# A two-layer transformer block on one core: six weight slots instead of four share the beginning with the first modulation

## The chip, the core and the metric

The kernel runs as one program on one core of a Trainium2 chip (trn2). The metric is the time of one execution in microseconds (us) of the device. The engines are TensorE (PE in the profile; its weight loads stand apart as PEld), VectorE (DVE), ScalarE (ACT), GpSimd (POOL) and SyncE (SP). Each engine takes its instructions in the order in which the program issued them; that order is written out by the kernel itself, since the code runs under a manual schedule. SP's queue issues nearly all transfers.

## What is computed

The reference is a transformer of two layers on 256 tokens of an image and 256 tokens of context, 1024 wide. Each layer has a half feed-forward step, an attention step and a second half feed-forward step. Nine vectors of modulation per layer come from a product of two conditioning vectors with `w_ada`. Cut to what the change touches:

```python
mod_x = (silu(c) @ w_ada[l] + b_ada[l]).reshape(bn, 1, N_MOD, d)
mod_c = (silu(c_ctx) @ w_ada[l] + b_ada[l]).reshape(1, 1, N_MOD, d)

def _half_ffn(h, g, shift, scale, gate, w_up, w_down):
    y = _rmsnorm(h, g) * (1 + scale) + shift
    a, b = split(y @ w_up, 2)            # w_up: 1024 x 5632
    return h + 0.5 * gate * ((silu(a) * b) @ w_down)

h_x = _half_ffn(h_x, norm_g[l, 0], mod_x[:, :, 0], mod_x[:, :, 1], mod_x[:, :, 2], ffn1_up[l], ffn1_down[l])
h_c = _half_ffn(h_c, norm_g[l, 0], mod_c[:, :, 0], mod_c[:, :, 1], mod_c[:, :, 2], ffn1_up[l], ffn1_down[l])
# then attention with mod 3, 4, 5 and the second half feed-forward with mod 6, 7, 8
```

All inputs are fp32, and the first up projection can't start before the shift and scale (modulation rows 0 and 1) of its first columns are known.

## The kernel before, in words

**Products.** Activations and weights are each kept as a high part (fp32r) and a low part, the remainder. A *unit product* is one TensorE instruction on a 128 x 128 weight tile and 512 tokens (256 in the parts that go by halves of the tokens). Three of them make one step of a projection's sum: high weight by high activation, high by low, low by high (`mm3`, L349 to L351). A projection of 1024 inputs has 8 such steps, so a column block of 128 outputs takes 24 unit products.

**Weight slots.** The weights come as a stream of loads of 1 MB (`raw`, three buffers, `RAW_BUFS`). One load makes two *slots* of 1024 columns: ScalarE casts the high part (L307), VectorE subtracts to get the low part (L310). Seven buffers hold slots (`W_BUFS`). `pump` casts ahead while fewer than six are out, `take` hands the next slot to a projection and casts it on the spot if it isn't there yet, `done` gives a slot back and pumps. What is cast ahead, and so where a cast stands on ScalarE and VectorE, is thus fixed when the program is built, by a count of slots that are out. For the first feed-forward, each load has 128 columns of both halves of `ffn1_up`, in rows of 512 bytes (`ffn_stream`).

**The planner's clock.** `tick` adds a planned duration to a clock of the program's own at every step of products, and runs what `later` has put off until then: the squares and sums for the norm of the next stage, pieces of modulation, refills. The place of such work in the engines' orders comes from this clock.

**The beginning.** Rows 0 and 1 of the modulation are computed in four *quarters* of 256 columns. A quarter has two loads of 1 MB (`quarter_load`, i = 0 and 1), two groups of four TensorE products (`quarter_ada`, L1306), a copy on ScalarE (L240), four transposes (`quarter_finish`, L1313), a reduction on VectorE (L1315) and then four modulations, for two chunks of 128 features and two sets of 256 tokens: VectorE makes the scaled value (L438), ScalarE the high part (L439), VectorE the low part (L433). A quarter so releases two of the eight steps of the up projection. `first` (L1356) handles the first four slots in this rhythm: the four PSUM banks of the `mm` pool hold one output block each, and quarters 1, 2 and 3 stand between the steps that are already released. The table `AT` says how many of the four blocks run ahead of a quarter's products and of its transposes. The four slots come out of the common stream (`take`): the transfers of the first two loads go to two pieces of the input buffer that are free by then (`extra`), and the two loads of quarter 0 stand ahead of both of them. `emit_split(lambda: quarter_finish(0, sb))` casts the first slot ahead of quarter 0's modulations.

**The other modulation rows.** Rows 2, 3, 4, 5 and 8 of layer 0 (`MODS[0]`) are accumulated during the first half feed-forward, one piece of 512 columns and 128 inputs at a time (`ada_one`: a load of 256 KB, and a multiply-add on VectorE, L222). `ada_step` is called after every up slot outside `first` and after every down slot: 40 times there (44 up slots without the first four) and 22 times in the down projections, 62 in all. Each call allows two pieces as long as the urgent row 2 is worked on, and 1.3 after that (`ADA_RATE`). When a row is complete, its sum across partitions, `ada_total` (L230), follows 22 us of the planner's clock later (`ADA_TOT`), 5 us for the urgent row. The accumulator lies in one of the seven slot buffers until that sum is made, so a fourth slot of what comes next can't be cast before it.

**The boundary to attention.** The last down chunks are followed by the squares (L375), the statistics (L411, L390 to L399) and the modulations of attention's operand, first for tokens 0 to 255, then for the rest. `attention` takes four slots at its start (L797).

```python
sl = [take() for _ in range(4)]     # L797, attention's first four slots
```

Of the kernel before, what the change touches and what calls it, by code (L numbers as in the profile page):

```python
# [32 lines left out]
AT = ((1, 2), (0, 1), (0, 1))  # L33
# [18 lines left out]
def dit_kernel(  # L52
# [515 lines left out]
    def ffn(a, gate, both, after, split_first, prep=None, mods=(), each=None):  # L568
# [4 lines left out]
        for pi, (f0, nf) in enumerate(FPARTS):  # L573
# [674 lines left out]
    ffn_stream(ffn1_up[0], ffn1_down[0])  # L1248
# [6 lines left out]
    with tc.manual_schedule():  # L1255
# [12 lines left out]
        extra += [xin[:, 4096:6144], xin[:, 6144:8192]]  # L1268

# [30 lines left out]
        def quarter_ada(h):  # L1300
# [3 lines left out]
            for i in range(2):  # L1304
                for j in range(4):
                    PE.matmul(out=ps[32 * j:32 * j + 32, :], lhsT=sc[:, 4 * i + j, :], rhs=raws[2 * h + i][:, j * 512:(j + 1) * 512],  # L1306
                              start=(i == 0), stop=(i == 1))
            return ada_rows(ps)

        def quarter_finish(h, sb):  # L1310
            tp = ps_ada.tile([128, 512], F32, tag="ada", name="ada")
            for q in range(4):
                PE.transpose(tp[:, q * 128:(q + 1) * 128], sb[:, q * 128:(q + 1) * 128], ident)  # L1313
            part = small.tile([128, 40], F32, tag="rs_t", name="part")[:, 0:8]
# [30 lines left out]
        sb = quarter_ada(0)  # L1345
# [3 lines left out]
        for v in range(2):  # L1349
            rstds[v] = r4[:, 2 * v:2 * v + 2]  # L1350
            ups.append(apply(v, 0, a["t"], None, spread(v, rb[:, v * TX:v * TX + TX])))
        raws += [quarter_load(1, 1, xv[:, 0:2].rearrange("p b d -> p (b d)")), quarter_load(2, 0, xv[:, 2:4].rearrange("p b d -> p (b d)"))]
        raws += [quarter_load(h, i, fresh()) for h, i in ((2, 1), (3, 0))]
        emit_split(lambda: quarter_finish(0, sb))

        def first():  # L1356

            ps = [mm_bank() for _ in range(4)]

            def dense(h, js):  # L1360
                for k in (2 * h, 2 * h + 1):
                    for j in js:
                        mm3(ps[j], [(wcol(sl[j], k, 0), acol(a["t"], k, 0, NT))], NT, k == 0, k == KD - 1)
            sl = [take() for _ in range(4)]
            for h in range(3):
                dense(h, range(0, AT[h][0]))
                sb = quarter_ada(h + 1)
                if h == 0:
                    raws.append(quarter_load(3, 1, fresh()))
                else:  # L1370
                    st["raws"] -= 1
                    loads()
                dense(h, range(AT[h][0], AT[h][1]))
                quarter_finish(h + 1, sb)
                dense(h, range(AT[h][1], 4))
            st["raws"] -= 1
            loads()
            for i in range(2):
                dense(3, (2 * i, 2 * i + 1))
                done(2)  # L1380
            return ps
# [117 lines left out]
```

## Time and profile before

| | |
|---|---|
| runs of the kernel before, us | 1706.02, 1703.14, 1705.49; median 1705.49 |
| the profiled execution, us | 1705.38 |
| its span in the trace, us | 1703.6 |
| mean granted clock of TensorE | 0.994 of full speed |
| TensorE busy | 1672.7 us, 98% |
| VectorE busy | 1037.6 us, 61% |
| ScalarE busy | 670.7 us, 39% |

The profiled execution's own time is 1.8 us longer than its span, which is what lies around the instructions. Busy times are sums over instructions; TensorE's matmuls overlap one another in the records, so a unit product shows about 0.36 us though one ends every 0.23. The 40 slices of the page show full busy shares nearly everywhere; the first slice is the one that stands out, with TensorE busy in six tenths of it, and the granted clock there in eight.

### The profile page before, as it was taken

How to read it: one execution, taken by the hardware profiler on the slowest of the kernel's cores; microseconds unless marked ns; L12 is line 12 of the kernel's file. 1: busy time of each engine (PE TensorE's matmuls, PEld its weight loads, DVE VectorE, ACT ScalarE, POOL GpSimd, SP SyncE). 2: the span in 40 equal slices, each digit the busy share in tenths (PEclk: the TensorE clock that was granted, in tenths of full speed). 3: DMA queues.
4: the chain of work that ended last, by engine and by line, in shares of the span. 5: the costliest groups of instructions: out<-in, count | busy, mean ns of one | idle time of the engine just before them, and what ended most of it. 6: DMA issues, size and time to landing. Idle time of an engine off the chain costs nothing.

```text
span 1703.6 us, 23729 instructions
## 1 busy us (share of the span) xinstructions
PE 1672.7 (98%) x9512; PEld 1417.9 (83%) x9512; DVE 1037.6 (61%) x1781; ACT 670.7 (39%) x1135; POOL 47.6 (3%) x67
## 2 busy tenths in 40 slices
PE   6999999999999999999999999999999999999998
PEld 4778888889886798888888898888888997799998
DVE  4666667567555676665764466545533657586674
ACT  4432222324556743323233243213222356674443
POOL 0000200000010000000000000020000000010000
PEclk8999999999999999999999999999999999999999
DMA  9745556432304325553653325565533224566561
GB/s 320 205 162 173 173 161 191 154 128 66 112 25 167 108 74 185 173 149 121 194 155 120 91 81 175 159 174 167 148 99 99 75 76 162 172 198 181 167 198 50
DMA packets 295335, 246.48 MB, mean 145 GB/s; under 512 B 9377, under 2 KB 262442, under 8 KB 293176
## 3 DMA queue, kind: packets, MB, share of 16 engines
q1 hardware_dynamic: 292680, 241.30, 45.8%
q0 software_dynamic: 1088, 2.15, 0.5%
q8 instruction: 75, 1.23, 0.3%
q10 hardware_dynamic: 1456, 1.52, 0.3%
q14 instruction: 36, 0.29, 0.1%
HBM read 243.88 MB, written 2.00 MB: 144 GB/s over the span
## 4 chain that ended last, share of the span: by engine, by line
PE 90%; DVE 4%; DMA 3%; ACT 2%; issue 1%; SPq 0%; DVEq 0%; ACTq 0%
PE mm L349 25%; PE mm L350 25%; PE mm L351 25%; PE mm L645 2%; PE mm L644 2%; PE mm L646 2%; PE mm L1010 1%; PE aux L976 1%; DMA ada_raw<-in_w_ada_dram 1%; DVE w L310 1%; PE ada L182 1%; PE mm L936 1%; DVE ada_acc L222 1%; PE mm L937 1%; PE ada L230 1%
## 5 line engine op out<-in xcount | busy, mean ns | idle before, releaser
L349 PE MATMUL mm<-act,w 128*128 128x512 f32 (+1 forms) x2240 | 809.8, 362 | 3.6 <-ACT act L439 2.1
L351 PE MATMUL mm<-act,w 128*128 128x512 f32 (+1 forms) x2240 | 802.7, 358 | 1.9 <-DVE w L310 1.9
L350 PE MATMUL mm<-act,w 128*128 128x512 f32 (+1 forms) x2240 | 802.9, 358 | 1.1 <-DVE act L433 0.9
L310 DVE TENSOR_TENSOR w<-raw,w 128x1024 fp32r<-128x1024 f32 (+1 forms) x311 | 369.9, 1198 | 219.4 <-ACT w L307 218.4
L349 PEld LDWEIGHTS mm<-act,w 128*128 128x128 f32 x2240 | 424.1, 189 | 84.8 <-issue 16.8
L351 PEld LDWEIGHTS mm<-act,w 128*128 128x128 f32 x2240 | 424.1, 189 | 64.2 <-DVE w L310 2.5
L350 PEld LDWEIGHTS mm<-act,w 128*128 128x128 f32 x2240 | 424.4, 189 | 62.8 <-DVE act L433 1.4
L307 ACT CAST w<-raw 128x1024 fp32r<-128x1024 f32 (+1 forms) x312 | 315.4, 1025 | 119.4 <-PE mm L351 96.9
L222 DVE SCALAR_TENSOR_TENSOR ada_acc<-ada_raw,sc,ada_acc 128x512 f32<-128x512 f32 x308 | 216.1, 746 | 50.3 <-DMA ada_raw<-in_w_ada_dram 26.2
L564 ACT CAST act<-gf 128x512 fp32r<-128x512 f32 x66 | 40.9, 620 | 275.5 <-DVE gf L561 275.5
L463 DVE SCALAR_TENSOR_TENSOR hT<-mm,hgt,hT 128x256 f32<-128x256 f32 x168 | 75.1, 480 | 95.9 <-PE mm L351 95.6
L558 ACT ACTIVATE sil<-mm 128x512 f32<-128x512 f32 x66 | 39.4, 597 | 185.5 <-PE mm L351 185.4
L645 PE MATMUL mm<-act,w 128*128 128x258 f32 x352 | 99.5, 283 | 0.3 <-DVE act L620 0.2
L644 PE MATMUL mm<-act,w 128*128 128x258 f32 x352 | 99.8, 284 | 0.0
L646 PE MATMUL mm<-act,w 128*128 128x258 f32 x352 | 99.3, 282 | 0.0
L561 DVE TENSOR_TENSOR gf<-sil,mm 128x512 f32<-128x512 f32 x66 | 45.2, 686 | 81.4 <-PE mm L351 70.8
L565 DVE TENSOR_TENSOR act<-gf,act 128x512 fp32r<-128x512 f32 x66 | 45.7, 693 | 45.3 <-ACT act L564 45.3
L645 PEld LDWEIGHTS mm<-act,w 128*128 128x128 f32 x352 | 66.8, 190 | 0.8 <-DVE act L620 0.8
L644 PEld LDWEIGHTS mm<-act,w 128*128 128x128 f32 x352 | 66.5, 189 | 0.0
L646 PEld LDWEIGHTS mm<-act,w 128*128 128x128 f32 x352 | 66.3, 188 | 0.0
L375 ACT ACTIVATE sq<-hT 128x256 f32<-128x256 f32 (+1 forms) x52 | 25.5, 490 | 102.5 <-DVE hT L463 102.2
L439 ACT ACTIVATE act<-nt,modT 128x256 fp32r<-128x256 f32 x80 | 39.5, 507 | 40.5 <-DVE nt L438 40.4
(171 smaller groups left out, 1163.4 us busy)
## 6 DMA issues: line engine op xcount, KB each, us to landing
raw<-in_ffn_up_dram SPq DMA_DIRECT2D x172, 512.0 KB
ada_raw<-in_w_ada_dram SPq DMA_DIRECT2D x192, 256.0 KB
raw<-in_ffn_down_dram SPq DMA_DIRECT2D x32, 1024.0 KB
raw<-in_w_ada_dram SPq DMA_DIRECT2D x16, 1024.0 KB
raw<-in_ffn_down_dram SPq DMA_DIRECT2D x16, 768.0 KB
raw<-in_w_in_dram SPq DMA_DIRECT2D x10, 1024.0 KB
raw<-in_w_out_dram SPq DMA_DIRECT2D x8, 1024.0 KB
raw<-in_w_ada_dram SPq DMA_DIRECT2D x12, 512.0 KB
```

What stands on the lines that cost most here:

```text
L222: DVE.scalar_tensor_tensor(out=o, in0=raw, scalar=col, in1=o, op0=ALU.mult, op1=ALU.add)
L307: ACT.copy(out=wh, in_=sl)
L310: eng.tensor_tensor(out=wl, in0=sl, in1=wh.bitcast(F32), op=ALU.subtract)
L349: PE.matmul(out=ps, lhsT=wh, rhs=ah, start=start and i == 0, stop=False)
L350: PE.matmul(out=ps, lhsT=wh, rhs=al, start=False, stop=False)
L351: PE.matmul(out=ps, lhsT=wl, rhs=ah, start=False, stop=stop and i == last)
L463: DVE.scalar_tensor_tensor(out=hT[:, k, cols], in0=ps, scalar=gate[:, k, v:v + 1], in1=hT[:, k, cols], op0=ALU.mult, op1=ALU.add)
L561: DVE.tensor_tensor(out=u[:, 0:n], in0=s[:, 0:n], in1=pb[:, 0:n], op=ALU.mult)
L565: DVE.tensor_tensor(out=gl, in0=uv, in1=gh.bitcast(F32), op=ALU.subtract)
L644: PE.matmul(out=ps[:, 0:NX], lhsT=wh, rhs=ah, start=k == 0, stop=False)
L645: PE.matmul(out=ps[:, 0:NX], lhsT=wh, rhs=al, start=False, stop=False)
L646: PE.matmul(out=ps[:, 0:NX], lhsT=wl, rhs=ah, start=False, stop=k == KD - 1)
```

## The change

`first` now handles six slots and not four: five banks of the `mm` pool and one of the `aux` pool hold the outputs (`ps6`), and the order of steps is written out by hand.

- **Loads.** The first two loads of the stream are 256 columns of each half of `ffn1_up`, in rows of 1 KB (`ffn_stream(..., wide=2)`); each makes two slots of one half. The loads of blocks and of quarters alternate: block 0 stands ahead of quarter 1, block 1 between the two loads of quarter 1 and quarter 2, block 2 (still 512-byte rows) ahead of quarter 3. `block(2)` reuses the buffer of block 0, so it waits for the casts of slots 0 and 1.
- **Casts.** `early_part` casts part of a slot: 256 columns (two of eight steps) and then 768 for slots 0 to 3, twice 512 for slots 4 and 5. The first slots' parts stand in front of quarter 0's modulations, not the whole first slot. Slots 2 and 3 are cast behind quarter 1's modulations, slots 4 and 5 behind quarter 2's.
- **TensorE's order.** The products of two blocks alternate (`dense`), and quarter 1 comes after 12 of them, as before after 12 of two blocks. `busy(n)` puts n small products of the identity with itself at five places of the beginning (4, 2, 8, 2 and 8 of them); their result is overwritten. The factors of the norm (`factors`, the transposes of the reciprocal roots) stand between the two halves of quarter 0.
- **The rest of the feed-forward.** `first` yields three pairs of banks; after each pair's evacuation `done(2)` gives two slots back. Two more slots pass without an `ada_step`, so 60 calls are left of 62.

```diff
-AT = ((1, 2), (0, 1), (0, 1))
...
             if "products" in a and pi == 0:
-                pss = a["products"]()
-                for i in range(2):
-                    up_evac(pss[2 * i], pss[2 * i + 1], g, i, 1, 0, n)()
-                m = 2
+                for pa, pb in a["products"]():
+                    up_evac(pa, pb, g, m, 1, 0, n)()
+                    done(2)
+                    m += 1
...
-    def ffn_stream(up, down):
+    def ffn_stream(up, down, wide=0):
...
+        for o in (0, DFF) if wide else ():
+            add_main(up[:, o:o + 256].rearrange("(k p) f -> p k f", p=128), (KD, 256), [c0, c1])
         for f0, nf in FPARTS:
-            for fj in range(f0 * 128, (f0 + nf) * 128, 128):
+            for fj in range((f0 or wide) * 128, (f0 + nf) * 128, 128):
...
-        raws = [quarter_load(0, i, fresh()) for i in range(2)]
-        loads()
-        raws.append(quarter_load(1, 0, fresh()))
+        def block(i):
+            extra.append(xin[:, 4096 + i % 2 * 2048:6144 + i % 2 * 2048])
+            emit_load()
+        raws = {(0, i): quarter_load(0, i, fresh()) for i in range(2)}
+        block(0)
+        raws[1, 0] = quarter_load(1, 0, fresh())
...
+        def busy(n):
+            for _ in range(n):
+                PE.matmul(out=ps6[-1][:, 0:128], lhsT=ident, rhs=ident, start=True, stop=True)
...
+        def early_part(j, k0, k1):
+            sl = slots[("raw", j // 2)][:, 0:2048].rearrange("p (k c) -> p k c", k=KD)[:, k0:k1, j % 2 * 128:(j % 2 + 1) * 128]
...
+            ACT.copy(out=wh, in_=sl)
+            return lambda: DVE.tensor_tensor(out=wl, in0=sl, in1=wh.bitcast(F32), op=ALU.subtract)
...
-        emit_split(lambda: quarter_finish(0, sb))
+        sb = quarter_ada(0, factors)
+        busy(2)
+        raws[1, 1] = quarter_load(1, 1, xv[:, 0:2].rearrange("p b d -> p (b d)"))
+        block(1)
+        raws[2, 0] = quarter_load(2, 0, xv[:, 2:4].rearrange("p b d -> p (b d)"))
+        raws[2, 1] = quarter_load(2, 1, fresh())
+        low0, low1 = early_part(0, 0, 2), early_part(1, 0, 2)
+        low0()
+        quarter_finish(0, sb, 8)
+        low1()
+        early_pair(0, 2, KD)
+        block(2)
+        raws[3, 0] = quarter_load(3, 0, fresh())
...
+            dense(0, 0, 1)
+            sb = quarter_ada(1)
+            raws[3, 1] = quarter_load(3, 1, fresh())
+            busy(2)
+            quarter_finish(1, sb, 8)
+            early_pair(2, 0, 2)
+            early_pair(2, 2, KD)
+            dense(1, 0, 1)
+            dense(0, 2, 3)
+            sb = quarter_ada(2)
...
+            dense(1, 2)
+            quarter_finish(2, sb)
+            early_pair(4, 0, 4)
+            early_pair(4, 4, KD)
+            dense(1, 3)
+            dense(0, 4, 5)
+            dense(2, 0, 1)
+            sb = quarter_ada(3)
...
+            dense(1, 4)
+            quarter_finish(3, sb)
+            dense(1, 5)
+            dense(2, 2, 3)
+            dense(2, 4, 5)
...
+            for pa, pb in ((0, 2), (1, 3), (4, 5)):
+                dense(3, pa, pb)
+                yield ps6[pa], ps6[pb]
```

**How the orders differ.** The first place is ScalarE's order from the casts behind quarter 0 to quarter 2's modulations, in the kernel before. The names `w_` are slots, `xin` and `raw` the buffers of the loads, `adasb` the copy of a quarter, `act` the first operand's high parts.

```order
L307 CAST w_265<-xin_103 128x1024
L307 CAST w_268<-xin_103 128x1024
L307 CAST w_271<-xin_103 128x1024
L240 COPY adasb_289<-ada_280 128x512
L439 ACTIVATE act_217<-nt_309,modT_94 128x256
L439 ACTIVATE act_217<-nt_312,modT_94 128x256
L439 ACTIVATE act_217<-nt_315,modT_94 128x256
L439 ACTIVATE act_217<-nt_319,modT_94 128x256
L240 COPY adasb_346<-ada_337 128x512
L439 ACTIVATE act_217<-nt_366,modT_94 128x256
```

In the kernel before, the casts of slots 1 to 3 stand ahead of quarter 1's copy, and no cast stands between the quarters. In the changed kernel the place from quarter 2's copy on reads:

```order
L239 COPY adasb_392<-ada_383 128x512
L438 ACTIVATE act_203<-nt_412,modT_94 128x256
L438 ACTIVATE act_203<-nt_415,modT_94 128x256
L438 ACTIVATE act_203<-nt_418,modT_94 128x256
L438 ACTIVATE act_203<-nt_422,modT_94 128x256
L1330 CAST w_428<-xin_103 128x512
L1330 CAST w_430<-xin_103 128x512
L1330 CAST w_428<-xin_103 128x512
L1330 CAST w_430<-xin_103 128x512
L239 COPY adasb_477<-ada_468 128x512
```

The four casts of slots 4 and 5 (`w_428`, `w_430`) stand behind all four modulations of quarter 2 and ahead of quarter 3's copy.

The second place is TensorE's order around quarter 2 in the changed kernel; `mm_206` and `mm_207` are the outputs of slots 2 and 3, `mm_208` and `aux_209` those of slots 4 and 5.

```order
L1404 MATMUL mm_207<-act_203,w_351 128x512
L1310 MATMUL ada_383<-xin_103,sc_93 32x512 x4
L1310 MATMUL ada_383<-raw_236,sc_93 32x512 x4
L1404 MATMUL mm_206<-act_203,w_349 128x512 x6
L1340 MATMUL ada_403<-ident_85,adasb_392 128x128 x4
L1404 MATMUL mm_207<-act_203,w_351 128x512 x6
L1404 MATMUL mm_208<-act_203,w_428 128x512
L1404 MATMUL aux_209<-act_203,w_430 128x512
```

Six products stand on either side of the transposes, and the products that come next are those of slots 4 and 5 with quarter 0's features. In the kernel before, the products behind quarter 2's transposes (L1313) were those of slots that had been cast before quarter 1.

The third place is ScalarE's order at the end of the first half feed-forward, in the kernel before. `sq` are the squares of the last down chunks, `w_2820`, `w_2853`, `w_2888` and `w_2915` attention's first four slots, `adasb_2913` is the copy of the fifth modulation row's sum.

```order
L307 CAST w_2820<-raw_2641 128x1024
L375 ACTIVATE sq_2851<-hT_84 128x512
L307 CAST w_2853<-raw_2641 128x1024
L375 ACTIVATE sq_2886<-hT_84 128x512
L307 CAST w_2888<-raw_2717 128x1024
L240 COPY adasb_2913<-ada_2907 128x512
L307 CAST w_2915<-raw_2717 128x1024
L375 ACTIVATE sq_2931<-hT_84 128x256
L375 ACTIVATE sq_2960<-hT_84 128x256
```

The same place in the changed kernel; attention's first four slots are `w_2851`, `w_2886`, `w_2921` and `w_3074`, the fifth is `w_3142`, and `adasb_3140` is the copy of the fifth row's sum.

```order
L374 ACTIVATE sq_2980<-hT_84 128x256
L374 ACTIVATE sq_3027<-hT_84 128x256
L438 ACTIVATE act_3039<-nt_3043,modT_94 128x256
L438 ACTIVATE act_3039<-nt_3055,modT_94 128x256
L438 ACTIVATE act_3039<-nt_3066,modT_94 128x256
L374 ACTIVATE sq_3071<-hT_84 128x256
L306 CAST w_3074<-raw_2738 128x1024
L438 ACTIVATE act_3039<-nt_3098,modT_94 128x256
L438 ACTIVATE act_3039<-nt_3132,modT_94 128x256
L438 ACTIVATE act_3039<-nt_3136,modT_94 128x256
L239 COPY adasb_3140<-ada_3108 128x512
L306 CAST w_3142<-raw_2817 128x1024
```

The fourth cast has moved behind the last square and into the modulations, and the fifth row's copy and a fifth cast have moved behind six modulations.

## Rows read from the trace of the kernel before

**Rows 1.** Part 1 of the page: busy time, share of the span, instructions.
```profile
PE 1672.7 (98%) x9512; PEld 1417.9 (83%) x9512; DVE 1037.6 (61%) x1781; ACT 670.7 (39%) x1135; POOL 47.6 (3%) x67
```

**Rows 2.** Stretches: length, busy PE, PEld, DVE, ACT, POOL, clock, DMA share, GB/s.
```profile
13.00:17.80 4.80, 3.12 (x24) 1.02 (x16) 1.85 (x12) 1.74 (x3) 0.00 (x0) 1.00 1.15 307
17.80:22.19 4.39, 1.02 (x3) 0.37 (x2) 4.19 (x12) 3.15 (x7) 0.00 (x0) 1.00 1.16 298
18.00:19.00 1.00, 0.00 (x0) 0.00 (x0) 0.90 (x5) 0.15 (x2) 0.00 (x0) 1.00 1.16 290
22.19:32.43 10.24, 7.81 (x25) 3.18 (x26) 4.19 (x4) 2.42 (x3) 0.00 (x0) 0.50 1.10 348
32.43:40.00 7.57, 7.57 (x46) 4.89 (x45) 3.85 (x11) 2.40 (x5) 0.00 (x0) 1.00 1.06 334
...
1379.11:1384.11 5.00, 3.80 (x32) 3.55 (x30) 1.69 (x4) 3.99 (x11) 0.00 (x0) 1.00 0.00 0
1384.11:1390.94 6.83, 6.37 (x28) 5.77 (x27) 6.31 (x11) 3.36 (x5) 1.57 (x1) 0.50 0.62 174
```

**Rows 3.** TensorE's waits, 10 to 60 us: releaser, total us, times, longest.
```profile
PE mm L349 <- ACT act L439: 2.1, 1, 2.1
```

**Rows 4.** TensorE's timeline: start, us, instructions, in brackets idle before and releaser.
```profile
15.40 1.07 PE L1306 MATMUL ada<-raw,sc 128*32 128x512 f32 x8 [1.56 <-DMA raw<-in_w_ada_dram]
...
28.62 1.93 PE L1306 MATMUL ada<-xin,sc 128*32 128x512 f32 x8 [1.12 <-DMA xin<-in_w_ada_dram]
...
32.88 0.60 PE L1313 MATMUL ada<-ident,adasb 128*128 128x128 f32 x4
33.23 0.47 PE L349 MATMUL mm<-act,w 128*128 128x512 f32 x1
33.54 0.39 PE L350 MATMUL mm<-act,w 128*128 128x512 f32 x1
...
35.83 0.39 PE L351 MATMUL mm<-act,w 128*128 128x512 f32 x1
36.15 1.06 PE L1306 MATMUL ada<-xin,sc 128*32 128x512 f32 x8
...
38.00 0.50 PE L349 MATMUL mm<-act,w 128*128 128x512 f32 x1
```

**Rows 5.** Timeline of all engines around the boundary to attention, 394 to 412 us.
```profile
394.64 1.06 PE L230 MATMUL ada<-ada_acc,ones 128*32 128x512 f32 x8
...
396.25 1.05 ACT L307 CAST w<-raw 128x1024 fp32r<-128x1024 f32 x1
...
397.34 1.23 DVE L310 TENSOR_TENSOR w<-raw,w 128x1024 fp32r<-128x1024 f32 x1
...
405.06 0.36 PE L349 MATMUL mm<-act,w 128*128 128x256 f32 x1
...
408.44 0.42 ACT L375 ACTIVATE sq<-hT 128x256 f32<-128x256 f32 x1 [0.28 <-DVE hT L463]
...
409.71 0.16 DVE L390 TENSOR_SCALAR rs_v<-aux 128x2 f32<-128x2 f32 x1 [0.52 <-PE aux L411]
...
411.66 0.16 DVE L399 SCALAR_TENSOR_TENSOR rs_y<-rs_t,rs_y 128x2 f32<-128x2 f32 x1
```

**Rows 6.** Timeline of quarter 0 (17.86, 19.95) and quarter 2 (40.16, 42.88).
```profile
17.86 0.19 DVE L1315 TENSOR_REDUCE part<-ada 128x8 f32<-128x32 f32 x1 [2.66 <-PE ada L1313]
...
19.95 0.50 PE L349 MATMUL mm<-act,w 128*128 128x512 f32 x1 [2.14 <-ACT act L439]
...
40.16 0.19 DVE L1315 TENSOR_REDUCE part<-ada 128x8 f32<-128x32 f32 x1 [2.67 <-PE ada L1313]
...
42.88 1.27 DVE L433 SCALAR_TENSOR_TENSOR act<-nt,modT,act 128x256 fp32r<-128x256 f32 x3
```

**Rows 7.** Part 5 of the page: count, busy us, mean ns, idle time before.
```profile
L565 DVE TENSOR_TENSOR act<-gf,act 128x512 fp32r<-128x512 f32 x66 | 45.7, 693 | 45.3 <-ACT act L564 45.3
```

**Rows 8.** TensorE's waits, 60 to 420 us.
```profile
PE ada L230 <- DVE ada_acc L222: 0.8, 1, 0.8
```

More of the change, by code (lines that the diff above doesn't have):

```diff
@@ L1305, in quarter_ada, with early_pair, quarter_finish @@
                 for j in range(4):
-                    PE.matmul(out=ps[32 * j:32 * j + 32, :], lhsT=sc[:, 4 * i + j, :], rhs=raws[2 * h + i][:, j * 512:(j + 1) * 512],
+                    PE.matmul(out=ps[32 * j:32 * j + 32, :], lhsT=sc[:, 4 * i + j, :], rhs=raws[h, i][:, j * 512:(j + 1) * 512],
                               start=(i == 0), stop=(i == 1))
+                if i == 0 and between:
+                    between()
             return ada_rows(ps)
-        def quarter_finish(h, sb):
+        def busy(n):
+            for _ in range(n):
+                PE.matmul(out=ps6[-1][:, 0:128], lhsT=ident, rhs=ident, start=True, stop=True)
+        early = []
+        def early_part(j, k0, k1):
+            sl = slots[("raw", j // 2)][:, 0:2048].rearrange("p (k c) -> p k c", k=KD)[:, k0:k1, j % 2 * 128:(j % 2 + 1) * 128]
+            if len(early) == j:
+                w = wp.tile([128, 2, 1024], F32R, tag="w", name="w")
+                early.append(tuple(w[:, i].rearrange("p (k c) -> p k c", k=KD) for i in range(2)))
+            wh, wl = (w[:, k0:k1] for w in early[j])
+            ACT.copy(out=wh, in_=sl)
+            return lambda: DVE.tensor_tensor(out=wl, in0=sl, in1=wh.bitcast(F32), op=ALU.subtract)
+        def early_pair(j, k0, k1):
+            for low in [early_part(j, k0, k1), early_part(j + 1, k0, k1)]:
+                low()
+        def quarter_finish(h, sb, n=0):
             tp = ps_ada.tile([128, 512], F32, tag="ada", name="ada")
@@ L1313, in quarter_finish @@
                 PE.transpose(tp[:, q * 128:(q + 1) * 128], sb[:, q * 128:(q + 1) * 128], ident)
+            busy(n)
             part = small.tile([128, 40], F32, tag="rs_t", name="part")[:, 0:8]
@@ L1344, in dit_kernel @@
         r4 = rsqrt(squares[:, 0:4], 4, 1.0 / D)
-        sb = quarter_ada(0)
         rb = aux_bank()
@@ L1348, in dit_kernel @@
         ups = []
[L1349 to L1353, printed above, removed]
-        emit_split(lambda: quarter_finish(0, sb))
+        ps6 = [mm_bank() for _ in range(5)] + [aux_bank()]
@@ new lines, in factors @@
+        def factors():
+            busy(4)
+            for v in range(2):
+                rstds[v] = r4[:, 2 * v:2 * v + 2]
+                ups.append(apply(v, 0, a["t"], None, spread(v, rb[:, v * TX:v * TX + TX])))
+        sb = quarter_ada(0, factors)
[4 more added lines that the diff above has]
+        raws[2, 1] = quarter_load(2, 1, fresh())
@@ L1356, in first, with dense @@
+        low0, low1 = early_part(0, 0, 2), early_part(1, 0, 2)
[5 more added lines that the diff above has]
+        raws[3, 0] = quarter_load(3, 0, fresh())
         def first():
-            ps = [mm_bank() for _ in range(4)]
-            def dense(h, js):
+            def dense(h, *js):
                 for k in (2 * h, 2 * h + 1):
-                    for j in js:
-                        mm3(ps[j], [(wcol(sl[j], k, 0), acol(a["t"], k, 0, NT))], NT, k == 0, k == KD - 1)
@@ L1364, in first @@
[L1364 to L1375, printed above, removed]
+                    for x, y in ((0, 0), (1, 0), (0, 1)):
+                        for j in js:
+                            PE.matmul(out=ps6[j], lhsT=early[j][x][:, k], rhs=a["t"][:, y, k, :], start=k + x + y == 0, stop=k == KD - 1 and y == 1)
+                            tick(MM[NT])
@@ new lines, in first @@
+            quarter_finish(2, sb)
[5 more added lines that the diff above has]
+            sb = quarter_ada(3)
+            st["raws"] -= 2
+            loads()
+            dense(1, 4)
[3 more added lines that the diff above has]
+            dense(2, 4, 5)
+            for i in range(3):
+                slots.pop(("raw", i))
+            st["split"], st["nslot"], st["take"] = 3, 6, 6
@@ L1382, in dit_kernel @@
+            st["out"] += 6
+            for pa, pb in ((0, 2), (1, 3), (4, 5)):
+                dense(3, pa, pb)
+                yield ps6[pa], ps6[pb]
         a["products"] = first
```

9 lines of the change are left out of this document (2 added, 7 removed).

## The prediction

> **What bounds the kernel now.** I read the busy times of the page first: TensorE is busy 98% of the span [rows 1]. So almost nothing is to be had except where TensorE waits or runs slowly, and the change works on such a place, the first 70 us. There I read the stretches cut at the clock's changes [rows 2]: from 17.80 to 22.19 TensorE was busy 1.02 us, then the granted clock is 0.50 (1.2 GHz) for 10.24 us, after which it is 1.00 (2.4 GHz). The waits of TensorE name what ended the longest idle times there: the first activations (2.1 us) [rows 3] and a late load (1.12, in brackets at 28.62) [rows 4]. The timeline of TensorE gives the count that I use. The 13th unit product starts at 33.23; products then follow every 0.228 us (10 from 33.54 to 35.83); a quarter of the modulation takes 1.85 us (36.15 to 38.00), its four transposes 0.6 [rows 4]. With no further wait, 132 products, two quarters and two groups of transposes end the six slots at 33.2 + 30.1 + 3.7 + 1.2 = 68.2 us. That is the mark to beat. The time after it is TensorE's; only what moves a wait there counts.
>
> **The loads.** The second half of quarter 0 lands at 15.40 [rows 4]. Behind it the transfers run without a break, at 348 GB/s for rows of 1 KB and 290 where weights come in rows of 512 bytes [rows 2]; that is 3.0 or 3.6 us for 1.05 MB. The new order then lands the first wide block at 18.4, quarter 1 at 21.4 and 24.4, the second block at 27.4, quarter 2 at 33.4, the third (still 512 bytes) at 37.0, quarter 3 at 43.0. SP's queue passes the third block only when VectorE has read the first (about 25.5), some 8 us before its turn. As will be seen, none is late.
> The Trainium skill (DMA: Bandwidth & Descriptors, Specifications) gives 512 B as the smallest transfer that reaches line rate. This trace does not agree: 290 against 348 GB/s. If the rule held and the lower rate had another cause, the first block would land at 19.0 and the end would come 0.6 us later.
>
> **The beginning, step by step.** ScalarE and VectorE take their rows in order. The parts of the first slots (256 columns, 0.42 us by the nearest operation of that size [rows 5]) now stand ahead of quarter 0's modulations and wait for the whole block, where before the first cast had gone ahead. So: 18.4 + 0.42 + 0.42 = 19.2 for the reduction (before 17.86), and 2.09 us from there to the first product [rows 6], 21.3 (before 19.95). The fourth product needs the second weight's low part, which stands behind eight modulations: reduction + 3.99 [rows 6] + 0.42 = 23.6. Nine more products end at 25.65, quarter 1 (landed) at 27.5. From a quarter's end to its first product (15.40 + 1.07 to 19.95 before) it takes 3.5 us [rows 4, 6], in which the order now holds only the transposes and fillers: 31.0. This is 2.2 us ahead of the 33.23 of before. The ten fillers there cost nothing unless one takes over 0.29 us; a transpose of the same size takes 0.15, and a plain fp32 product counts as two in the profile (8 for 4 in a quarter's half), so 0.15 to 0.3, and I take nothing.
> Then 24 products, a 0.3 us wait for a low part, and quarter 2: 38.6. Six products, transposes, six products: 42.0. Here comes the loss. The fifth and sixth slots are cast behind quarter 2's four activations on ScalarE, and their low parts behind its modulations on VectorE, though their block landed at 37.0. The transposes end and the reduction starts at 40.65, the modulations end 3.99 later [rows 6], two low parts of 512 columns take 0.62 each (half of one of 1024 [rows 5]) to 0.69 [rows 7], some 1.3: the fourth of these products starts at 45.95. TensorE has done three in 3.95 us: 3.3 us lost. The rest is work without waits: 9 products 48.0, 12 products 50.75, quarter 3 52.6, twice six and transposes 55.9, 24 products 61.4, the last 36 at 69.6. **+1.4 us** against 68.2.
> To this the clock. Before, 1.02 us of work in 4.39 was followed by 1.2 GHz, and it rose again only 3.8 us after TensorE had become continuous at 28.62 [rows 2, 4]. The stall at 42 leaves TensorE 0.7 us of work in 3.95, so I expect a second fall at about 46. Bounds: nothing, or half of the 6.83 us that the other low stretch of the trace lasted, 3.4 [rows 2]. I take half of 3.8, the nearest to such a stop: **+1.9 us**.
>
> **The sums of modulation.** Two more slots pass without an ada_step: 60 steps are left of 62 in the first half-FFN. Five rows of modulation need 8 steps at two pieces and 64/1.3 = 49 more, so the fifth sum is complete after step 58 in both kernels. It is two slots (2 x 24 x 0.228 = 10.9 us) nearer to the end, and stands 22 us of the planner's clock behind that. The first sum made TensorE wait 0.8 us [rows 8]. VectorE gets its pieces later now, behind the down weights on SP; bounds 0 and twice that wait more, and I take **+0.8**.
> The fifth sum stood at 394.64, ahead of the last two down slots, and gave back a weight buffer, so a fourth cast followed at 396.25 and its low part at 397.34 [rows 5]. Moved by 10.9 us and what the start loses it stands behind attention's first products, as the order shows. So only three of attention's first four slots are cast ahead; the fourth is cast when taken, behind the square at 408.44 of the last down chunk. On the clock of before: attention's first product starts at 406.9 (15 products of 0.12 behind 405.06); the tenth needs the fourth slot at 408.0. It gets the high part at 408.44 + 0.42 + 1.05 = 409.9 (1.9 us late) and the low part 1.23 later (1.1 us more) [rows 5]. Giving back the buffer then triggers a fifth cast and low part in the middle of the second half's modulations, which another product waits for: 1.23 (the low part) to 2.3 (with the cast), I take 1.8. And the reciprocal root of that half (409.71 to 411.82) [rows 5] loses part of its cover of 18 products: 0 to 2.1, I take 0.7. That is 1.9 + 1.1 + 1.8 + 0.7 = 5.5. And the clock may fall there: at 1384.11 it did, after 5 us with TensorE busy 3.80 [rows 2]; bounds again 0 and 3.4, I take 1.5. **+7.0**, bounds 3.0 (only the fourth slot) and 11 (all of it).
>
> **Sum.** 1.4 + 1.9 + 0.8 + 7.0 = 11.1 us. The profiled execution took 1705.38 (1703.6 span); the median, 1705.49, is the same to 0.1. Forecast: **1716.5 us**, its own range 1711.5 to 1722.
>
> **Rivals.** (1) *The boundary holds*: the fifth sum falls back ahead of the last slots, or the fourth cast is hidden. Then only the beginning and the first sum count: 1705.4 + 4.1 = 1709.5. Against it: the order of ScalarE.
> (2) *The beginning is won, the boundary lost*: the stall at 42 is short and the clock stays up. Then 2.2 us gained by product 13 stay gained, less 0.3: -1.9 + 0.8 + 7.0, 1711.3. For it: quarter 1 is in memory 4 us earlier than TensorE got it before.
> (3) *Ready casts pass waiting activations on ScalarE*, the one mechanism that ends not slower. At 42 it takes away 3.3 + 1.9, at the boundary all 7.0; left is -1.9 + 0.8 = -1.1: 1704.3, and with a first sum without a wait and the low first clock fully won back (12 products and a quarter at half rate before, some 4 us of which 2.2 are already counted) 1701.5. It decides if the fifth slot's cast starts before quarter 2's last activation. Against it: in before the second weight's cast runs only after the activations. The Trainium skill (TensorE: Matmul & The Clock Gate, Part 1) calls ScalarE's queue strict FIFO, and this trace agrees.
> (4) *The fillers don't hold the clock.* In the kernel before it fell after 3.80 us of work in 5.00, and stayed after 3.12 in 4.80, a smaller share [rows 2]; so the busy time of the rows does not tell. If it falls before quarter 1, that quarter (+1.9) and 12 products (+2.4) run at 1.2 GHz: 1720.8. The same section of the Trainium skill says that the default state is throttled and that activity releases it; what counts as activity for narrow fp32 fillers no run here shows.
>
> **How the numbers follow.** Chances: forecast 0.52, (1) 0.11, (2) 0.11, (3) 0.18, (4) 0.08. A measurement of this kernel tells about 0.2%, 3.4 us, from no change (the runs shown spread by 0.17%). All but (3) are slower by more than that: 0.82. Of (3), whose times straddle -0.2%, I give 0.11 to no change and 0.07 to faster. The range reaches down past (1) and (2) with their bounds, to 1708, which leaves out (3), and up to 1722, which takes in (4) and the upper bounds in part.
>
> **What would show it.** Right: the fifth slot's first unit product waits some 3 us for its cast at 42 to 46; PEclk 0.50 for a few us behind it; no low clock from 22 to 32; the 13th product near 31; a wait of TensorE on ScalarE's cast and on the low part near 410, none of which before had; and nothing lost after 430. Wrong: the six slots ending before 68 us, four casts ahead of attention's first product, or a loss in a stage that this working does not name.

## The result and the profile after

| | before | changed |
|---|---|---|
| median of five executions, us | 1704.42 | 1721.25 |
| lowest to highest, us | 1702.98 to 1706.02 | 1713.40 to 1723.66 |
| ratio, 95% interval | | 1.0092 [1.0078, 1.0105] |
| the profiled execution and its span, us | 1705.38, 1703.6 | 1721.25, 1719.5 |

The change is slower by 0.92%, some 16 us. 1721.25 lies inside the range, 4.75 us above the forecast of 1716.5. The spans of the two profiled executions differ by 15.9 us, and the traces say where these come up. First the page's busy times of the changed kernel, which answer to [rows 1]:

```profile
PE 1683.4 (98%) x9560; PEld 1426.5 (83%) x9560; DVE 1037.6 (60%) x1787; ACT 671.1 (39%) x1141; POOL 47.3 (3%) x67
```

The share of TensorE is 98% as before, and says nothing. The stretches of the changed kernel, cut where the granted clock changes, answer to [rows 2] (length, busy times of the five engines, clock, DMA share, GB/s):

```profile
10.49:44.62 34.13, 28.02 (x174) 18.42 (x172) 19.50 (x55) 13.83 (x29) 0.00 (x0) 1.00 1.11 338
44.62:48.04 3.42, 3.29 (x8) 2.35 (x9) 2.62 (x5) 1.64 (x4) 0.00 (x0) 0.50 0.25 64
48.04:123.13 75.09, 73.01 (x331) 57.99 (x329) 46.59 (x66) 25.41 (x36) 0.00 (x0) 1.00 0.55 176
123.13:129.96 6.83, 5.99 (x14) 3.46 (x15) 2.98 (x4) 3.97 (x6) 0.00 (x0) 0.50 0.00 1
...
416.68:420.09 3.41, 3.13 (x13) 1.25 (x13) 1.01 (x3) 0.51 (x1) 0.00 (x0) 0.50 0.50 140
420.09:450.81 30.72, 27.62 (x214) 26.47 (x214) 16.75 (x47) 15.94 (x37) 0.00 (x0) 1.00 0.07 20
450.81:454.22 3.41, 3.41 (x9) 2.67 (x9) 3.16 (x3) 3.05 (x4) 1.56 (x1) 0.50 0.15 33
```

The low clock of before at 22 us is gone in this execution, and four new low stretches have come, of which the first three begin during waits that before did not have. (Both traces have a low stretch of 6.83 us late in the kernel, at 1384.11 [rows 2] and at 1399.72, and one at the very end.) The waits of TensorE, 10 to 70 us (answering to [rows 3]):

```profile
PE mm L1404 <- ACT w L1330: 2.6, 1, 2.6
PE mm L1404 <- ACT act L438: 1.9, 2, 1.6
PE mm L1404 <- DVE w L1331: 1.3, 1, 1.3
```

and 70 to 420 us (answering to [rows 8], which had one wait of 0.8 in that whole stage):

```profile
PE ada L229 <- DVE ada_acc L221: 2.9, 1, 2.9
PE mm L348 <- ACT w L306: 1.7, 1, 1.7
PE mm L350 <- DVE w L309: 0.8, 1, 0.8
```

Set beside each other by equal work, the traces give the account of the 15.9 us. Each pair of rows has before first and the changed kernel second:

```profile
68.40 0.39 PE L349 MATMUL mm<-act,w 128*128 128x512 f32 x1
70.78 0.39 PE L348 MATMUL mm<-act,w 128*128 128x512 f32 x1
...
137.63 0.88 DVE L463 SCALAR_TENSOR_TENSOR hT<-mm,hgt,hT 128x256 f32<-128x256 f32 x2 [1.43 <-PE mm L351]
144.90 0.88 DVE L462 SCALAR_TENSOR_TENSOR hT<-mm,hgt,hT 128x256 f32<-128x256 f32 x2 [2.11 <-PE mm L350]
...
431.20 1.50 ACT L812 CAST K<-mm 64x256 fp32r<-64x256 f32 x4 [3.86 <-PE mm L351]
445.12 1.12 ACT L813 CAST K<-mm 64x256 fp32r<-64x256 f32 x3 [4.15 <-PE mm L350]
```

The 145th unit product with 512 tokens, the first behind the six slots, starts at 68.40 before and at 70.78 after: **+2.4**. The third residual of the first down projection (VectorE's addition to `hT`) starts at 137.63 and 144.90, so **+4.9** between the six slots and there: the first modulation sum and the low clock behind it. ScalarE's third group of key casts in attention starts at 431.20 and 445.12: **+6.6** more, at the boundary. The low stretch from 450.81 adds 3.41 at half rate, **+1.7**. That is 15.6 of 15.9, and 13.9 without the last item, which will turn out not to belong to the change.

The place in the beginning, from the timeline of the changed kernel:

```profile
41.47 1.26 DVE L437 SCALAR_TENSOR_TENSOR nt<-hT,gsc,aux 128x256 f32<-128x256 f32 x3
...
43.68 0.51 ACT L438 ACTIVATE act<-nt,modT 128x256 fp32r<-128x256 f32 x1 [0.39 <-DVE nt L437]
44.10 2.16 ACT L1330 CAST w<-xin 128x512 fp32r<-128x512 f32 x4
...
44.75 0.79 PE L1404 MATMUL mm<-act,w 128*128 128x512 f32 x1 [2.56 <-ACT w L1330]
```

ScalarE starts the casts at 44.10, behind quarter 2's last activation, though the last packet of their block had ended at 36.9. TensorE waits 2.56 us. At the boundary:

```profile
414.29 0.42 ACT L374 ACTIVATE sq<-hT 128x256 f32<-128x256 f32 x1 [0.28 <-DVE hT L462]
414.62 1.03 ACT L306 CAST w<-raw 128x1024 fp32r<-128x1024 f32 x1
415.67 1.23 DVE L309 TENSOR_TENSOR w<-raw,w 128x1024 fp32r<-128x1024 f32 x1 [1.42 <-ACT w L306]
415.69 0.39 PE L348 MATMUL mm<-act,w 128*128 128x256 f32 x1 [1.68 <-ACT w L306]
416.96 0.58 PE L350 MATMUL mm<-act,w 128*128 128x256 f32 x1 [0.76 <-DVE w L309]
418.11 1.94 PE L229 MATMUL ada<-ada_acc,ones 128*32 128x512 f32 x8
```

The fourth slot's cast follows the last square, its low part follows the cast, and the fifth row's sum, which stood at 394.64 before [rows 5], stands behind both. The first sum, from TensorE's timeline:

```profile
120.00 1.05 PE L229 MATMUL ada<-ada_acc,ones 128*32 128x512 f32 x4
123.97 1.92 PE L229 MATMUL ada<-ada_acc,ones 128*32 128x512 f32 x4 [2.92 <-DVE ada_acc L221]
```

Its second half waits 2.92 us for VectorE's last multiply-adds, and the clock falls at 123.13, while it waits.

### The profile page after: what moved, and what is told of

Read it like the earlier page. It is cut to its first block, busy times and chain, and to the rows that moved or that the text cites. A ratio compares the mean times of both kernels' runs of the same rounds, so it can differ in the third digit from the quotient of the medians.

```text
span 1719.5 us, 23840 instructions
## 1 busy us (share of the span) xinstructions
PE 1683.4 (98%) x9560; PEld 1426.5 (83%) x9560; DVE 1037.6 (60%) x1787; ACT 671.1 (39%) x1141; POOL 47.3 (3%) x67
## 4 chain that ended last, share of the span: by engine, by line
PE 89%; DVE 5%; ACT 2%; DMA 2%; issue 1%; SPq 0%; DVEq 0%; ACTq 0%
PE mm L348 24%; PE mm L350 24%; PE mm L349 24%; PE mm L644 2%; PE mm L643 2%; PE mm L645 2%; PE mm L1011 1%; PE mm L1404 1%; PE aux L977 1%; DMA ada_raw<-in_w_ada_dram 1%; DVE w L309 1%; PE ada L181 1%; PE ada L229 1%; PE mm L937 1%; DVE ada_acc L221 1%
## 5 line engine op out<-in xcount | busy, mean ns | idle before, releaser
L348 PE MATMUL mm<-act,w 128*128 128x512 f32 (+1 forms) x2192 | 791.4, 361 | 3.1 <-ACT w L306 1.7
L349 PE MATMUL mm<-act,w 128*128 128x512 f32 (+1 forms) x2192 | 785.1, 358 | 1.0 <-DVE act L432 0.9
L350 PE MATMUL mm<-act,w 128*128 128x512 f32 (+1 forms) x2192 | 784.7, 358 | 1.2 <-DVE w L309 1.2
L348 PEld LDWEIGHTS mm<-act,w 128*128 128x128 f32 x2192 | 415.8, 190 | 79.7 <-issue 13.4
L350 PEld LDWEIGHTS mm<-act,w 128*128 128x128 f32 x2192 | 415.9, 190 | 61.8 <-DVE w L309 1.7
L349 PEld LDWEIGHTS mm<-act,w 128*128 128x128 f32 x2192 | 416.1, 190 | 61.1 <-DVE act L432 1.3
L560 DVE TENSOR_TENSOR gf<-sil,mm 128x512 f32<-128x512 f32 x65 | 44.6, 686 | 87.3 <-PE mm L350 70.6
L644 PEld LDWEIGHTS mm<-act,w 128*128 128x128 f32 x352 | 66.8, 190 | 0.8 <-DVE act L619 0.8
L643 PEld LDWEIGHTS mm<-act,w 128*128 128x128 f32 x352 | 66.5, 189 | 0.0
L645 PEld LDWEIGHTS mm<-act,w 128*128 128x128 f32 x352 | 66.3, 188 | 0.0
```

Of the source, the lines that this page charges most:

```text
L348: PE.matmul(out=ps, lhsT=wh, rhs=ah, start=start and i == 0, stop=False)
L349: PE.matmul(out=ps, lhsT=wh, rhs=al, start=False, stop=False)
L350: PE.matmul(out=ps, lhsT=wl, rhs=ah, start=False, stop=stop and i == last)
L560: DVE.tensor_tensor(out=u[:, 0:n], in0=s[:, 0:n], in1=pb[:, 0:n], op=ALU.mult)
L643: PE.matmul(out=ps[:, 0:NX], lhsT=wh, rhs=ah, start=k == 0, stop=False)
L644: PE.matmul(out=ps[:, 0:NX], lhsT=wh, rhs=al, start=False, stop=False)
```

## The experiments

Ratios are to the kernel before on the same chip. An interval is some 2 us to either side, so a difference of two of these ratios is known to some 3 us; each run has one trace, of one of its executions. The theory after the two traces: three places cost the time, each by a wait and the low clock behind it, and they can be mended one by one. The rivals: the waits move elsewhere, or the clock falls whatever is done.

### e1: the fifth sum earlier

```diff
-            later(5.0 if m == st["urgent"] else ADA_TOT[st["ffn"]], lambda: ada_total(m, acc))
+            later(5.0 if m == st["urgent"] else 8.0 if m == 8 else ADA_TOT[st["ffn"]], lambda: ada_total(m, acc))
```

> The changed kernel, with the fifth modulation row's sum put off by 8 us of the planner's clock instead of 22. Theory (three places): the boundary to attention lost 6.7 us because that sum gave its buffer back too late. Now it stands ahead of the last down slots again, four slots are cast ahead, the waits on the fourth slot's cast (1.7) and low part (0.8) and the low clock from 416.7 go: 1721.25 - 6.7 = 1714.6, and 1712.9 if the low clock from 450.8 (3.4 us at half rate) goes as well. Rival (VectorE is late at any place): the earlier sum finds VectorE's multiply-adds unfinished and makes TensorE wait there instead: 1718 to 1721. Rival (the clock falls by chance): the waits go and the low stretches stay: 1716.3.

Measured: 1710.77 (1706.84 to 1716.67) against 1704.89 before, ratio 1.0038 [1.0025, 1.0051]; the changed kernel had 1.0092, so 9.2 us come back by the ratios and 10.5 by the medians. TensorE's waits from 400 to 435 us are gone altogether, and the stretch from 50.83 us to almost the end is at full clock (its profile, columns as above):

```profile
47.41:50.83 3.42, 3.42 (x9) 2.51 (x8) 1.47 (x3) 0.49 (x1) 0.00 (x0) 0.50 0.00 0
50.83:1702.00 1651.17, 1637.73 (x9358) 1394.19 (x9356) 1011.67 (x1719) 650.30 (x1101) 44.06 (x59) 1.00 0.46 140
```

The boundary's loss belongs to the place of that one sum. The first rival falls. The second falls for the median, not for every execution: the eight lie 9.8 us apart, with mean clocks from 0.998 to 0.992, and the profiled one (1708.57) is the second fastest. What comes back beyond the expected 8.4 is less than the uncertainty. A single trace doesn't give a sum here: this one also lacks the low stretch that before had at 1384 [rows 2], and has one at 23.52 that the changed kernel's trace lacks.

### e2: the first sum later

```diff
-            later(5.0 if m == st["urgent"] else ADA_TOT[st["ffn"]], lambda: ada_total(m, acc))
+            later(10.0 if m == 2 else 5.0 if m == st["urgent"] else ADA_TOT[st["ffn"]], lambda: ada_total(m, acc))
```

> The changed kernel, with the first row's sum put off by 10 us of the planner's clock instead of 5. Theory (three places): the sum came 2.9 us before VectorE had its last multiply-adds done, and the wait was followed by 6.83 us at 1.2 GHz; put behind them it waits for nothing, and the place that lost 4.8 us against before loses nothing: 1721.25 - 5.6 = 1715.6 (before's 0.8 goes too). Rival (the gate is late): the columns of the gate come too late for the first down products, and VectorE's residuals and TensorE's banks wait there: 1719 to 1723. Rival (the clock falls by chance): the wait goes, a low stretch comes elsewhere: 1718.4.

Measured: 1715.51, ratio 1.0057 [1.0044, 1.0071]; 5.7 us less than the changed kernel by the medians and 6.0 by the ratios, where 5.6 was expected. TensorE waits for nothing from 60 to 200 us, and the clock doesn't fall there. The gate (the columns that this row's sum yields) was in time.

### e3: the casts of slots 4 and 5 earlier

```diff
-            quarter_finish(2, sb)
             early_pair(4, 0, 4)
+            quarter_finish(2, sb)
```

> The changed kernel, with the first halves of slots 4 and 5 cast ahead of quarter 2's modulations instead of behind them. Theory (order of ScalarE): their block landed at 37.5, two casts of 512 columns and two low parts are done before the transposes end at 40.6, so the wait of 2.6 at 44.75 and the low clock behind it (3.4 us at half rate, 1.7) go: 1721.25 - 4.3 = 1717. Rival (the cast only moves the wait): the copy of quarter 2 and its reduction wait for the casts and low parts, quarter 2's features come some 2 us later and the products that need them wait: 1719 to 1721.

Measured: 1713.17, ratio 1.0053 [1.0040, 1.0065]. The six slots end at 67.95 instead of 70.78 in its trace, with no wait on a cast. By the ratios it is 6.6 us better than the changed kernel, against 4.3 expected, which is within the uncertainty; the profiled execution was the slowest of its five (1717.59), so its trace can't show if there is more. It shows another thing, in TensorE's waits from 60 to 200 us:

```profile
PE ada L229 <- DVE ada_acc L221: 3.9, 1, 3.9
```

The first sum's wait depends on when TensorE comes: 1.1 us in e1's trace (six slots end at 72.95), 2.9 in the changed kernel (70.78), 3.9 here (67.95). TensorE reaches the sum at 122.17, 120.00 and 117.17 in these traces, 5.0 us apart; its second half starts, when VectorE is ready, at 124.34, 123.97 and 122.08, only 2.3 us apart. So this wait takes back part of whatever the beginning wins.

### e4: all three

The edits of e1, e2 and e3 together.

> The changed kernel with all three edits together. Theory (three places, independent of each other): 1721.25 - 8.4 - 5.6 - 4.3 = 1703, level with before (1704.4) or a little under it. Rival (the places are not independent, and where one wait goes another takes its place): 1707 or more. Rival (a low clock comes by chance in any order): two falls or more left in the first 500 us, 1706 to 1708.

Measured: 1702.14 (1699.39 to 1703.66) against 1704.89, ratio 0.9984 [0.9975, 0.9993]. With the three places mended the whole loss is gone. From its stretches:

```profile
22.55:25.97 3.42, 2.90 (x7) 2.32 (x8) 2.20 (x4) 0.95 (x2) 0.00 (x0) 0.50 1.09 346
25.97:1381.06 1355.09, 1350.23 (x6990) 1121.33 (x6989) 813.08 (x1360) 489.81 (x793) 31.11 (x47) 1.00 0.45 138
```

With the waits the low stretches behind them go too. A short one at 22.55 is left in the beginning, and behind 1381.06 the one that before has at 1384.11.

### e5: e4 without the fillers

```diff
         def busy(n):
-            for _ in range(n):
+            for _ in range(0):
```

> The kernel of e4 without the 24 small products (they are written nowhere; the computation is whole). Theory (the fillers shorten the low clock): e4's trace has 3.4 us at 1.2 GHz from 22.6, before had 10.24 from 22.2; the fillers were 5.9 us of TensorE's work between 16 and 31 (8 of them take 1.95). Without them the low stretch is 7 to 10 us long again, at most 6.8 us more at half rate, of which the waits for activations hide a part: 1702.1 + 1.7 to 3.4 = 1703.8 to 1705.5. Rival (TensorE waits there for activations anyway): the low clock changes nothing that ends last: 1702.1. Rival (the fillers stand in the way): 1701.

Measured: 1706.07 against 1704.91, ratio 1.0007 [0.9998, 1.0016], 3.9 us above e4. The stretches of its beginning:

```profile
22.64:29.47 6.83, 6.22 (x21) 3.41 (x25) 2.29 (x4) 1.03 (x2) 0.00 (x0) 0.50 1.10 349
32.88:39.70 6.82, 5.87 (x14) 4.62 (x15) 5.30 (x11) 3.87 (x8) 0.00 (x0) 0.50 1.13 322
```

Two low stretches of 6.8 us for one of 3.4, though this is the trace of the slowest of eleven executions (1709.04). By the medians the fillers are worth 3.9 us in the six-slot start, a little more than the expected 1.7 to 3.4, and without them it wins nothing over before. They shorten the low clock; they don't always prevent it, as e4's stretch at 22.55 shows.

### e6: the wide rows alone, on the kernel before

```diff
-    ffn_stream(ffn1_up[0], ffn1_down[0])
+    ffn_stream(ffn1_up[0], ffn1_down[0], 2)
...
-                    up_evac(pss[2 * i], pss[2 * i + 1], g, i, 1, 0, n)()
+                    up_evac(pss[i], pss[2 + i], g, i, 1, 0, n)()
...
-                dense(3, (2 * i, 2 * i + 1))
+                dense(3, (i, 2 + i))
```

with `wide` in `ffn_stream` as in the change.

> The kernel before with the first two loads as 256 columns of one half each (rows of 1 KB), four slots, the old order of work; only the pairs of banks follow the slots. Theory (the rows' width is worth what the rates say): 1.05 MB in 3.0 instead of 3.6 us, twice, lands the second half of quarter 1 some 1.2 us earlier; the wait of 1.12 at 28.62 goes, 1704.9 - 1.1 = 1703.8, and if TensorE, without a break from 26.7 on, gets its clock back one step earlier, up to 1.7 more: 1702.1. Rival (something else ends last at quarter 1): the wait stays and moves to another releaser: 1704.9.

Measured: 1703.03 against 1704.91, ratio 0.9991 [0.9982, 1.0000]: 1.9 us by the medians, at the edge of what can be told. In its trace the six slots' work ends at 66.03, 2.4 us ahead of before. Stretches and the second half of quarter 1:

```profile
18.00:19.00 1.00, 0.00 (x0) 0.00 (x0) 0.93 (x3) 0.95 (x1) 0.00 (x0) 1.00 1.10 349
22.22:29.05 6.83, 5.89 (x21) 1.66 (x21) 4.05 (x4) 1.69 (x2) 0.00 (x0) 0.50 1.10 348
```

```profile
27.10 1.94 PE L1308 MATMUL ada<-xin,sc 128*32 128x512 f32 x8 [0.24 <-DMA xin<-in_w_ada_dram]
```

349 GB/s instead of the 290 of rows of 512 bytes, the quarter 1.5 us earlier than [rows 4], and the low stretch 3.4 us shorter, as expected. The first sum's wait of 0.8 [rows 8] is gone from this trace as well.

### e7: the kernel before with its fifth sum late

```diff
-            later(5.0 if m == st["urgent"] else ADA_TOT[st["ffn"]], lambda: ada_total(m, acc))
+            later(5.0 if m == st["urgent"] else 33.0 if m == 8 else ADA_TOT[st["ffn"]], lambda: ada_total(m, acc))
```

> The kernel before with the fifth modulation row's sum put off by 33 us of the planner's clock instead of 22, and nothing else. Theory (the sum's place alone makes the boundary's loss): three slots cast ahead of attention as in the changed kernel, waits on the fourth slot's cast and low part near 406, and the low clock behind them: 1704.9 + 2.5 (the two waits) to + 8.4 (all that the changed kernel lost from 400 to 454), most likely + 5 to + 7: 1710 to 1712. Rival (the loss needs the six-slot start, by its later loads or its two missing steps): 1706 or less.

Measured: 1710.06 (1706.61 to 1712.06) against 1704.91, ratio 1.0030 [1.0018, 1.0041], +5.2 us, the lower end of what was thought most likely. TensorE's waits, 400 to 435 us:

```profile
PE mm L349 <- ACT w L307: 1.7, 1, 1.7
PE mm L351 <- DVE w L310: 0.8, 1, 0.8
```

The changed kernel's two waits appear in the kernel before, to a tenth of a microsecond. No six slots are needed for them: the sum's place is the cause. The smaller waits that followed in the changed kernel (0.8, 0.6 and 0.4 us) do not appear in this trace, which is that of the fastest of six executions; so it accounts for most of the boundary's 6.6 us, not for all of it.

### e8: four slots with wide rows and the later first sum

e6 with e2's edit.

> The kernel of e6 with the first row's sum put off by 10 us of the planner's clock instead of 5: four slots, with those parts of e4 that need no six slots. Theory (six slots are worth nothing by themselves): the wait of 0.8 on VectorE's multiply-adds goes as well: e6 - 0.8, 1701.3 to 1703, level with e4 (1702.1) or under it. Rival (the six-slot start is what makes e4 faster than before): 1704 or more, 2 us behind e4.

Measured: 1700.92 (1698.65 to 1702.74) against 1704.91, ratio 0.9978 [0.9969, 0.9987]. This is 0.22% faster than before and the fastest version of the study by its median. What was expected of the sum rested on a wait of 0.8 that e6's trace no longer has; the medians of e6 and e8 differ by 2.1, which is about as much as they can tell. Its interval overlaps that of e4: once the three places are mended, the six-slot start has brought nothing that can be told from four slots with wide rows.

### e9: e8 with fillers

```diff
-        emit_split(lambda: quarter_finish(0, sb))
+        busy(2)
+        emit_split(lambda: quarter_finish(0, sb, 8))
```

with `busy` as in the change, writing the fifth bank of `mm`.

> The kernel of e8 with ten small products of the identity between quarter 0's products and the first unit product (2 behind the quarter, 8 behind its transposes), into the one bank that is free there. Theory (the fillers shorten the low clock, as between e4 and e5): in e8's trace 6.83 us at 1.2 GHz start at 20.6, of which the unit products from 20.2 to 24.6 and a half of quarter 1 pay; with 3.4 us or none of it 1 to 2.5 us come back: 1698.4 to 1700. Rival (what ends last there are the activations and the low part of the first slot, 2.4 and 1.1 us of waits in e8): no difference, 1700.9.

Measured: 1701.23 against 1704.26, ratio 0.9982 [0.9973, 0.9991]; no difference to e8. The forecast gain didn't come, but not for the rival's reason alone: the clock did stay up,

```profile
10.94:1379.68 1368.74, 1357.26 (x7036) 1125.56 (x7035) 822.62 (x1382) 494.72 (x800) 31.14 (x47) 1.00 0.45 140
```

and TensorE then waited for the load instead:

```profile
24.22 1.06 PE L1308 MATMUL ada<-raw,sc 128*32 128x512 f32 x8
27.13 1.07 PE L1308 MATMUL ada<-xin,sc 128*32 128x512 f32 x8 [1.84 <-DMA xin<-in_w_ada_dram]
```

The second half of quarter 1 starts at 27.13, at 27.35 in e8 with half the clock. With four slots the transfer ends last there, and the low clock was hidden under it.

### e10: the later first sum alone, on the kernel before

The edit of e2 on the kernel before.

> The kernel before with the first row's sum put off by 10 us of the planner's clock instead of 5, and nothing else. Theory (the edits add up): the wait of 0.8 goes, and with it the low clock that may follow it in some executions: e8 was 2.1 us faster than e6, so 1704.9 - 2.1 = 1702.8, at least - 0.8, 1704.1. Rival (the later sum helps only where the loads come earlier): 1704.9.

Measured: 1704.30 against 1704.26, ratio 0.9997 [0.9988, 1.0006]: no difference. In its trace the place itself gains 1.9 us (the first residual of the down projection starts at 130.98, before at 132.87), more than the wait of 0.8. The sum's rows, the first two of before and the last of e10, show why:

```profile
106.74 1.05 PE L230 MATMUL ada<-ada_acc,ones 128*32 128x512 f32 x4
108.61 1.05 PE L230 MATMUL ada<-ada_acc,ones 128*32 128x512 f32 x4 [0.81 <-DVE ada_acc L222]
...
112.16 1.06 PE L230 MATMUL ada<-ada_acc,ones 128*32 128x512 f32 x8
```

The eight instructions take 1.06 us together, and 2.92 in two halves with the wait between them. A low stretch of 3.41 us from 435.23, which before did not have, takes 1.7 back. So the edits don't add up to e8's 4.0 in a way that these runs settle.

## Why the prediction was right, and where it was short

**The loads and the first quarters: right.** The first unit product starts at 20.93 (21.3 predicted), the 13th at 30.90 (31.0), quarter 2 ends at 38.7 (38.6). No load was late. (Among the longest idle times of before the prediction left out 1.4 us for the first slots' low part; its count starts behind it and doesn't use it.) The rows of 512 bytes were the slower ones, as the trace of before said: e6 has 349 GB/s in the second where before had 290, and shows what the wide rows are worth by themselves. The Trainium skill (DMA: Bandwidth & Descriptors, Specifications) names 512 B as enough for the full rate; the measurement decides against it here.

**The stall at 42: right in cause, off in detail.** The prediction let three products run and the fourth wait for its low part at 45.95, a loss of 3.3 us. In fact the first already waits, 2.56 us, for the high part; the fourth starts at 46.29. The clock fell at 44.6 and not at 46, for 3.41 us; up to 46.29 the casts and low parts set the pace, and behind them only four products ran slowly, from 46.29 to 48.00, in 1.7 us instead of 0.9. So the fall cost 0.8, where 1.9 was taken, and together the beginning cost 2.4 where 3.3 was forecast. e3 shows the cause: casts moved ahead of the modulations, the stall is gone. Rival (3), casts that pass activations, is refuted by the row at 44.10. Rival (4), fillers that don't hold the clock, did not come in the profiled execution, but it is not refuted. The programs of e1 to e4 are the same as the changed kernel's up to quarter 2, and in all four traces the clock fell for 3.4 us among the first products, ahead of quarter 1 (at 23.52, 23.62, 24.03 and 22.55); e1's stretch:

```profile
23.52:26.93 3.41, 3.41 (x9) 2.39 (x8) 1.45 (x2) 0.19 (x1) 0.00 (x0) 0.50 1.10 349
```

There the 13th product came at 32.1 to 32.6, 1.2 to 1.7 us later, not the 4.3 of (4). That 31.0 was met without a low clock from 22 to 32 is in part the luck of the execution that was profiled.

**The first sum: the term that was mis-sized.** The step is "bounds 0 and twice that wait more, and I take +0.8". It measured +4.9: the wait was 2.9, 2.1 more than before and beyond the upper bound of 1.6, and, the larger part, it was followed by 6.83 us at 1.2 GHz. The prediction priced a fall of the clock behind the other two stalls, but left it out behind this one. e2 gives the price: 5.7 us for the whole place. Why the wait grew shows in the row's first piece, on ScalarE, before and after:

```profile
71.33 1.34 ACT L220 ACTIVATE ada_acc<-ada_raw,sc 128x512 f32<-128x512 f32 x2 [6.63 <-DMA ada_raw<-in_w_ada_dram]
87.41 1.34 ACT L219 ACTIVATE ada_acc<-ada_raw,sc 128x512 f32<-128x512 f32 x2 [7.59 <-DMA ada_raw<-in_w_ada_dram]
```

The multiply-adds begin 16.1 us later, while TensorE reaches the sum 13.3 later (106.74 and 120.00). SP issues that first piece at 80.27 instead of 68.20, now right behind a load of down weights (79.86), and it takes 7.1 us from issue to use instead of 3.1. That is the reason that the prediction gave, with a larger size; no run tests it.

**The boundary: right.** Forecast +7.0, measured +6.6, and by the predicted parts: 1.7 on the cast (1.9 forecast), 0.8 on the low part (1.1), 0.75 on the reciprocal root (0.7), and 3.41 us of low clock (1.7 against 1.5); the fifth cast's wait among the modulations came to less than the 1.8 taken (0.6 and 0.4 us of waits). These parts add up to 5.9 of the 6.6. e1 and e7 show the cause from both sides.

**"Nothing lost after 430": wrong by 1.7.** A low stretch came at 450.81, behind a wait of 1.35 us for `ksq`, the squares of the keys, on ScalarE. Before has the same wait without a fall (first row before, second the changed kernel):

```profile
435.95 0.61 PE L850 MATMUL aux<-hind,ksq 128*128 128x2 f32 x4 [1.34 <-ACT ksq L871]
449.87 0.61 PE L851 MATMUL aux<-hind,ksq 128*128 128x2 f32 x4 [1.35 <-ACT ksq L872]
```

All twelve traces have this wait, with 1.34 to 1.36 us, and a fall of 3.41 us begins 0.9 to 1.3 us behind it in four of them: here, in e2, e5 and e10, the last without six slots. So it is not a place that the change touched, and these 1.7 us are not a price of the change; what decides there was not settled.

**The sum.** 3.3 + 0.8 + 7.0 became 2.4 + 4.9 + 6.6 + 1.7. The range held, by 0.75 us, since the surplus of the first sum was covered by its reach to cases with more low clock; two of the five executions lie above it.

## What to carry to other kernels

- Work that is taken out of a stage shifts whatever is counted in that stage's steps. Follow the last such item to the end of the stage and ask which buffer it holds: here one late sum cost 6.6 us, 350 us behind the edit.
- In a kernel that is bound by TensorE, price each new wait twice: the wait, and the low clock that may follow it. A row that shows a short wait in the trace of before gives the first price only, and a fall that lies under a wait costs only what is left of it behind the wait (0.8 us of 3.41 at 44.6).
- Try a bundle's parts alone. The wide rows and a later sum, a few lines on the old start, came out no slower than the six-slot start with its faults mended.

## What the runs showed that was not expected

The executions of the changed kernel lie 10.26 us apart, and their mean clocks tell almost all of it: 1713.40 with 0.996 and 1723.66 with 0.990. Time at half rate is twice the missing share, 13.7 and 34.4 us; half of the difference is 10.4. So the same waits cost a different amount from one execution to the next. The low stretches in the middle of the traces last 3.4 to 10.2 us, and one costs half of its length where TensorE has work. With small fp32 products of the identity the beginning had less low clock: none with them in e9's trace and 6.83 us without in e8's, 3.4 us with them in e4's and twice 6.8 without in e5's. That was worth time only where no transfer or activation ends last (3.9 us in the six-slot start, nothing with four slots).
